# Values half a block later, and the round trip of 1/z a block later, in the attention stage of a decoder trunk

## The chip, the cores and the metric

One core of one Trainium2 chip runs the whole trunk as one program. The metric is the device time of one execution in microseconds (us). Before the change it is 2227.3 us, the median of three runs (2226.78 to 2228.44).

The engines go by the names of the profile: PE is TensorE (matmuls), PEld its weight loads, DVE is VectorE, ACT is ScalarE, POOL is GpSimd, SP is SyncE. Each engine takes its instructions in order. DMAs are issued from the queues of SP, ACT and POOL. An instruction that waits for another engine or for a DMA holds up everything behind it on its own engine or queue.

## What is computed

Two decoder layers over 1024 positions of width 1024 in float32: a short gated convolution with a SwiGLU FFN, then dilated attention with 16 heads of 64 and a second FFN, and a last RMSNorm. The change is in the attention layer:

```python
qkv = (h @ w_qkv).reshape(bsz, seq, 3, N_HEADS, HEAD_DIM)
q, k, v = qkv[:, :, 0], qkv[:, :, 1], qkv[:, :, 2]
for window, dilation in BRANCHES:          # (128, 1), (512, 4), (2048, 16)
    o, l = dilated_branch(q, k, v, rel_bias, window, dilation)
    ...
alpha = jax.nn.softmax(jnp.stack(lses, axis=0), axis=0)
o = jnp.sum(alpha[..., None] * jnp.stack(outs, axis=0), axis=0)
return o.reshape(bsz, seq, D_MODEL) @ w_out
```

The weighted sum of three softmaxes is one softmax over all the scores of the three branches. So per head the kernel needs the exponentials of all scores below one common maximum, their products with the values, the sum z of the exponentials, and a division by z. Then comes the output product with `w_out` and the addition to the residual x.

## The kernel before

All engines follow an order that the source writes out by hand. Matrix products in float32 are made of three products of rounded parts (`hi` and `lo`), so weights and activations are split first: ACT copies the high part (L141), DVE subtracts (L142).

The kernel has stages: convolution, first FFN, query and key products of pairs 0 to 5 by Strassen-like products, attention, second FFN. A pair is two heads. The attention stage (`attention`, L1465) begins with the values of group 0 (`value_tiles`, two tiles) and the strided key copies of head 0 (`classes`, L1539, on ACT). Then `slot` (L1721) is called 17 times, once for each head n and once more. In what follows a call of `slot` is a block; it is even or odd as n is.

A block before the change works like this:

- SP loads the bias of head n+1 (L1451, L1452) and its keys and queries (`load_kq`, L1529 to L1533: `ka`, `qa`, `ql`).
- First half: eight steps of `scores` of head n on PE (L1555, L1556), evicted with the bias by DVE (L1566 to L1597), with the maximum over keys at the end (DVE L1605, L1606, and on POOL `partition_all_reduce`, L1609, into `mb`). Between them run the products with the values of head n-1 (`values`, PE L1628), which need the exponentials `lf`, `lh`, `ld`, `lp` and the values `vx`. At their end ACT copies z and o out of PSUM (L1651, L1652).
- Second half, eight steps: mostly `dense` work, that is steps of other products that fill PE: value tiles of groups 1 to 3 (L1500 to L1502), query and key products of pairs 6 and 7 (`projections`, L369 to L371), and at last the output product over the first five pairs (`out_product`, L369 to L371). A block has 15 dense steps, the last four blocks 20. In step 1 and 2 are the key copies of head n+1; in step 4 (`SOFT`) the softmax of head n: DVE subtracts `mb` (L1617), ACT takes the exponential (L1618). In even blocks `load_values` (L1512) loads `vx` of the pair on SP; there is one buffer of it, so the load waits for the values of the pair before.
- 1/z: the sum z lies along the free dimension in two partitions. In the second half of an even block `finish` (L1655) writes z of the last pair to HBM (L1660), reads it back with 128 partitions (`zc`, L1663), has DVE take the reciprocal (L1665), writes it (L1666), and reads it back spread over 64 partitions a head (L1668). All four DMAs are on POOL. In step 2 of the next odd block `attended` (L1711) multiplies o with 1/z on DVE (L1715) and stores o (L1716).

A value tile's evictions are ACT's (L1505), and its store to HBM too (L1509). The stage's `first` part of the output product adds into x, which SP loads (L1797). The rest of the pairs follow in `group1` of the next stage (`by_columns`), once the last head is divided. `AO` says how many pairs go into the first part.

Of the kernel before, what the change touches and what calls it, by code (L numbers as in the profile page):

```python
# [17 lines left out]
S = 1024  # L18
D = 1024
DF = 2816  # L20
H = 16
# [24 lines left out]
SOFT = 4  # L46
FIN0 = 2
AO_WIDE = 5
AO = 5
FILL = (("v", 0), ("v", 1), ("v", 2), ("qk", 6), ("v", 3), ("qk", 7))  # L50
DEEP_ORDER = (1, 2, 5, 6, 7, 3, 4)


# [44 lines left out]
def trunk(ctx: ExitStack, tc: tile.TileContext, x, gains_in, cwi, ck, cwo, wqkv, wo, relb,  # L98
# [275 lines left out]
    def run(*gens):  # L374
        for _ in zip(*gens):
            pass
        for g in gens:
            for _ in g:
                pass
# [1085 lines left out]
    def attention(norm, qk):  # L1465
# [23 lines left out]
        def value_tiles(g, j):  # L1489

            if j == 0:
                wv[:] = [take(("v", g, i), 1) for i in range(2)]
            v = page("v")
            for b4 in range(4):
                t = 4 * j + b4
                b = bank()[:, :256]
                for k in range(KT):
                    (hi, lo), (whi, wlo) = qk.h[j][k], wv[k // 4]
                    a, c = slice(b4 * 128, b4 * 128 + 128), slice(k % 4 * 256, k % 4 * 256 + 256)
                    nc.tensor.matmul(b, hi[:, a], whi[:, c], start=k == 0, stop=False)  # L1500
                    nc.tensor.matmul(b, hi[:, a], wlo[:, c], start=False, stop=False)  # L1501
                    nc.tensor.matmul(b, lo[:, a], whi[:, c], start=False, stop=k == KT - 1)  # L1502
                    if k % 2:
                        yield
                nc.scalar.activation(v[:, b4 * 256:b4 * 256 + 256], b, AF.Identity, scale=norm.r[:, t:t + 1])  # L1505
                yield
            vd = vdram[g]
            for r in range(4):
                nc.scalar.dma_start(bass.AP(vd.tensor, vd.offset + (512 * j + r) * 256,  # L1509
                                          [[16 * 256, 32], [4 * 256, 4], [1, 256]]), v[32 * r:32 * r + 32])  # L1510

        def load_values(p):  # L1512
            src = vdram[p // 2]
            for a in range(2):
                off = src.offset + p % 2 * 128 + a * 64
                dims = slice(128 * a, 128 * a + 64)
                nc.sync.dma_start(vx[:, 0:8, dims], bass.AP(src.tensor, off, [[256, 128], [128 * 256, 8], [1, 64]]))
                for h in range(2):
                    nc.sync.dma_start(vx[:, 8 + 4 * h:12 + 4 * h, dims],
                                        bass.AP(src.tensor, off + 512 * 256 * h, [[1024, 128], [256, 4], [1, 64]]))  # L1520

        def load_kq(n):
# [12 lines left out]
        def classes(n):  # L1535

            KC[n] = page("kca", F32R)
            for h in range(2):
                nc.scalar.activation(KC[n][:, half(h)], view(KS[n], h * HALF, [[1, 4], [4, 128]]), AF.Copy)  # L1539
                yield  # L1540
# [114 lines left out]
        def finish(p):  # L1655

            o, z = OZ.pop(p)
            if p < NPAIR - 1:
                zd, rd = zdram[p]
                nc.gpsimd.dma_start(zd, z[0:65:64])  # L1660
                yield
                zc = scope["pool"].tile([128, 16], F32, name="zc", tag="zc", bufs=2)
                nc.gpsimd.dma_start(zc, bass.AP(zd.tensor, zd.offset, [[16, 128], [1, 16]]))  # L1663
                yield
                nc.vector.reciprocal(zc, zc)  # L1665
                nc.gpsimd.dma_start(bass.AP(rd.tensor, rd.offset, [[16, 128], [1, 16]]), zc)  # L1666
                yield
                nc.gpsimd.dma_start(z, bass.AP(rd.tensor, rd.offset, [[S, 2], [0, 64], [1, S]]))  # L1668
                yield
                put_off.append((p, o, z))  # L1670
                return

            zd, rd = zdram[p]
            wide = lambda t: bass.AP(t.tensor, t.offset, [[HALF, 2], [1, HALF]])
            thin = lambda t: bass.AP(t.tensor, t.offset, [[8, 128], [1, 8]])
            nc.gpsimd.dma_start(wide(zd), z[0:65:64, HALF:])
            zc = scope["pool"].tile([128, 8], F32, name="zl", tag="zl", bufs=1)
            nc.gpsimd.dma_start(zc, thin(zd))
            acts[p] = page("o_hi", F32R), page("o_lo", F32R)

            def scaled(c0, c1):
                q = slice(c0, c1)
                nc.vector.tensor_tensor(out=o[:, q], in0=o[:, q], in1=z[:, q], op=ALU.mult)

            def parts(h):
                split(o[:, half(h)], [t[:, half(h)] for t in acts[p]])

            for c in (0, 256):
                nc.vector.reciprocal(z[:, c:c + 256], z[:, c:c + 256])
                scaled(c, c + 256)  # L1690
                if c:
                    parts(0)
                    nc.scalar.activation(scratch, eps, AF.Sqrt)
                yield

            def rest():
                scaled(HALF, S)
                parts(1)

            last_part.append(rest)  # L1700
            yield
            ensure(ahead_ao + KT - AO_WIDE)
            nc.vector.reciprocal(zc, zc)
            nc.gpsimd.dma_start(thin(rd), zc)
            for a in range(2):
                nc.gpsimd.dma_start(z[64 * a:64 * a + 64, HALF:],
                                    bass.AP(rd.tensor, rd.offset + a * HALF, [[0, 64], [1, HALF]]))
            ensure(ahead_ao + KT - AO_WIDE + 4)
            yield
# [11 lines left out]
        def slot(n, dense, ndense, late=0, hook=iter(())):  # L1721

            def other(k):
                for _ in range(k):
                    next(dense, None)

            p, a = divmod(n, 2)
            if n < H:
                new = dict(bias=bias.pop(n))
                sc = scores(p, a, new)  # L1730
            else:
                sc = iter(())
            if n + 1 < H:
                bias[n + 1] = load_bias(n + 1)
                load_kq(n + 1)
            if n:
                q, b = divmod(n - 1, 2)
                if b == 0:
                    OZ[q] = page("o"), page("z")
                old = live.pop(n - 1)  # L1740
                old.update(o=OZ[q][0], z=OZ[q][1])
                pv = values(q, b, old)
            else:
                pv = iter(())
            extra = later = iter(())
            used = 0
            if a == 0 and n and not late:
                other(1)
                used += 1
            for i in range(8):  # L1750
                next(sc, None)
                next(pv, None)
                next(pv, None)
                if (i >= late if late else i < 3) and i % 2 == 0:
                    other(1)
                    used += 1
            run(sc)
            run(pv)
            if n + 1 < H:
                later = classes(n + 1)  # L1760
            if a == 0 and p:
                extra = finish(p - 1)
            if a == 0 and n < H:
                load_values(p)
            left = max(ndense - used, 0)
            for i in range(8):
                if a == 1 and i == 2:
                    attended()
                if i < FIN0 or i > SOFT:
                    next(extra, None)  # L1770
                if i in (1, 2):
                    next(later, None)
                if i == SOFT:
                    if n < H:
                        live[n] = new
                        run(softmax(new))
                if i >= SOFT:
                    next(hook, None)
                other(left * (i + 1) // 8 - left * i // 8)
            run(extra)  # L1780

        def load_attended(ps):
# [20 lines left out]
        X[:] = [None] * KT  # L1803
        bias = {0: load_bias(0)}
        load_kq(0)
        for j in range(2):
            run(value_tiles(0, j))
        run(classes(0))
        live = {}
        ahead_ao = [k for k, f in ops].index(("ao", 1, AO_WIDE - 1))  # L1810
        done, first = {}, {}
# [10 lines left out]
        def halves():  # L1822
            for q, t in done.items():
                first[q] = split(t)
                yield

        dense = fill()
        for n in range(H):
            if n == H - 4:
                done.update(load_attended(range(AO)))  # L1830
            hook = halves() if n == H - 4 else iter(())
            slot(n, dense, 20 if n > H - 4 else 15, 3 if n == H - 2 else 0, hook)
            run(hook)
        acts.update(split_attended(load_attended(range(AO, 7))))
        ensure(ahead_ao)
        slot(H, dense, 20)
        run(dense)
        return acts

# [198 lines left out]
```

## Time and profile before

| | us |
|---|---|
| median of three runs | 2227.3 |
| the profiled execution's own time | 2226.7 |
| its span, first to last instruction | 2224.7 |
| PE busy | 2125.2 |
| DVE busy | 1747.7 |
| ACT busy | 1007.3 |
| POOL busy | 234.5 |
| PE busy in the attention stage, 1118.5 to 1541.0 | 348.4 of 422.5 |
| mean granted clock there | 0.89 of full speed |

How to read the lines: a group of instructions is named by its line, engine, operation and tiles, out<-in. "A <- B: t, n, m" is a wait: A waited for B, t us in all, n times, m the longest. In a timeline a row has the start, the length, the engine and the instruction; brackets hold the idle time of the engine before it and what ended it. Stretches give the busy time of the engines, the granted clock of PE, the share of the 16 DMA engines that was busy, and the rate.

### The profile page before, as it was taken

To read this page: it belongs to the slowest core of one execution; us is meant where nothing else is said; L and a number is where in the kernel's file an instruction comes from. 1 tells how busy PE (TensorE), PEld (TensorE's weight loads), DVE (VectorE), ACT (ScalarE), POOL (GpSimd) and SP (SyncE) were. 2 spreads that over 40 slices of the span, in tenths; PEclk is the share of its full clock that TensorE was granted. 3 is DMA by queue.
4 is the path that set the end of the run, shared out by engine and by line. 5 is a ranking of instruction groups with operands and counts; after the bars stand their busy time and mean duration, and the time that the engine had idled before them with its cause. 6 is when DMAs were issued, how large, how long until landed. Compare 5 with 4: busy or idle time off the path is not lost.

```text
span 2224.7 us, 30938 instructions
## 1 busy us (share of the span) xinstructions
PE 2125.2 (96%) x11086; PEld 1823.8 (82%) x11086; DVE 1747.7 (79%) x3272; ACT 1007.3 (45%) x1848; POOL 234.5 (11%) x331
## 2 busy tenths in 40 slices
PE   9999999999999999999988777799999999999998
PEld 7788888888888888778888667688788888888887
DVE  8897679988888888689665554677898888888886
ACT  7433336434343554355444333434644444446435
POOL 1000000101010010002212121221001010101000
PEclk9999999999999999999999888899999999999999
DMA  7322643233333584326666554765322333367532
GB/s 218 86 86 76 222 147 86 90 105 105 106 104 112 198 232 140 123 96 203 212 152 160 137 140 119 202 181 177 81 95 100 109 105 105 109 198 220 173 97 76
DMA packets 152584, 304.92 MB, mean 137 GB/s; under 512 B 55102, under 2 KB 66606, under 8 KB 152432
## 3 DMA queue, kind: packets, MB, share of 16 engines
q1 hardware_dynamic: 107488, 201.94, 30.5%
q0 software_dynamic: 32704, 82.12, 11.5%
q10 hardware_dynamic: 12240, 18.90, 2.4%
q8 instruction: 88, 1.44, 0.3%
q14 instruction: 64, 0.52, 0.1%
HBM read 212.48 MB, written 83.05 MB: 133 GB/s over the span
## 4 chain that ended last, share of the span: by engine, by line
PE 82%; DVE 7%; DMA 6%; issue 3%; ACT 2%; POOL 1%; SPq 0%; ACTq 0%; DVEq 0%; POOLq 0%
PE bank L562 19%; PE bank L561 18%; PE bank L560 18%; DMA z<-rdram 3%; PE bank L1628 3%; PE bank L371 3%; PE bank L370 3%; PE bank L369 3%; PE bank L652 3%; PE bank L655 3%; PE bank L654 3%; DVE w L142 1%; PE bank L1556 1%; DVE b L553 1%; PE bank L1501 1%
## 5 line engine op out<-in xcount | busy, mean ns | idle before, releaser
L562 PE MATMUL bank<-b,w 128*128 128x512 f32 x1952 | 761.9, 390 | 5.9 <-DVE w L142 5.7
L560 PE MATMUL bank<-b,w 128*128 128x512 f32 x1952 | 764.2, 392 | 1.3 <-ACT w L141 1.1
L561 PE MATMUL bank<-b,w 128*128 128x512 f32 x1952 | 761.8, 390 | 2.6 <-DVE b L553 2.2
L562 PEld LDWEIGHTS bank<-b,w 128*128 128x128 f32 x1952 | 367.2, 188 | 86.0 <-DVE w L142 9.7
L561 PEld LDWEIGHTS bank<-b,w 128*128 128x128 f32 x1952 | 367.5, 188 | 79.6 <-DVE b L553 3.1
L560 PEld LDWEIGHTS bank<-b,w 128*128 128x128 f32 x1952 | 367.5, 188 | 78.3 <-ACT w L141 1.7
L141 ACT ACTIVATE w<-combo 128x512 fp32r<-128x512 f32 (+2 forms) x488 | 249.1, 540 | 230.7 <-DVE combo L189 207.3
L142 DVE TENSOR_TENSOR w<-combo,w 128x512 fp32r<-128x512 f32 (+2 forms) x488 | 277.7, 583 | 37.9 <-ACT w L141 37.2
L566 ACT ACTIVATE part<-bank 128x512 f32<-128x512 f32 x186 | 110.8, 596 | 390.1 <-PE bank L562 388.3
L142 DVE TENSOR_TENSOR w<-raw,w 128x512 fp32r<-128x512 f32 (+2 forms) x334 | 183.0, 569 | 35.9 <-ACT w L141 35.9
L570 DVE TENSOR_TENSOR part<-part,bank 128x256 f32<-128x256 f32 (+1 forms) x366 | 171.3, 499 | 31.1 <-PE bank L562 16.6
L141 ACT ACTIVATE w<-raw 128x512 fp32r<-128x512 f32 (+2 forms) x334 | 161.2, 525 | 45.1 <-PE bank L562 11.5
L369 PE MATMUL bank<-w_hi,w 128*128 128x512 f32 (+1 forms) x320 | 119.6, 374 | 0.0
L371 PE MATMUL bank<-w_hi,w 128*128 128x512 f32 (+1 forms) x320 | 117.8, 368 | 0.7 <-DVE w L142 0.7
L370 PE MATMUL bank<-w_lo,w 128*128 128x512 f32 (+1 forms) x320 | 117.7, 368 | 0.0
L790 DVE TENSOR_TENSOR x<-x,bank 128x512 f32<-128x512 f32 x136 | 93.4, 687 | 29.2 <-PE bank L562 29.2
L189 DVE TENSOR_TENSOR combo<-raw 128x512 f32<-128x512 f32 (+1 forms) x172 | 111.8, 650 | 0.0
L491 DVE TENSOR_TENSOR x<-x,bank 128x512 f32<-128x512 f32 (+1 forms) x104 | 66.3, 643 | 56.3 <-PE bank L371 55.7
L1628 PE MATMUL bank<-lf,vx 128*128 128x128 f32 x256 | 43.3, 324 | 53.4 <-ACT lf L1618 53.4
L553 DVE TENSOR_TENSOR b<-hin,b 128x512 fp32r<-128x512 f32 x126 | 79.8, 690 | 9.2 <-ACT b L552 9.1
L1628 PEld LDWEIGHTS bank<-lf,vx 128*128 128x128 f32 x256 | 39.9, 236 | 55.2 <-ACT lf L1618 54.9
L1500 PE MATMUL bank<-w_hi,b 128*128 128x256 f32 x256 | 76.3, 298 | 8.6 <-ACT w_hi L141 8.6
(252 smaller groups left out, 3688.9 us busy)
## 6 DMA issues: line engine op xcount, KB each, us to landing
hin<-part SPq DMA_DIRECT2D x126, 256.0 KB, 4.7
raw<-in_ffn_w_gate SPq DMA_DIRECT2D x44, 512.0 KB, 4.2
raw<-in_ffn_w_up SPq DMA_DIRECT2D x44, 512.0 KB, 4.6
part<-sum POOLq DMA_DIRECT2D x72, 256.0 KB, 2.3
raw<-in_ffn_w_down SPq DMA_DIRECT2D x48, 384.0 KB, 3.3
raw<-in_attn_w_qkv SPq DMA_DIRECT2D x27, 512.0 KB, 3.8
raw<-in_conv_w_in SPq DMA_DIRECT2D x24, 512.0 KB, 3.6
part<-part POOLq DMA_DIRECT2D x36, 256.0 KB, 2.4
```

The source lines that it names most:

```text
L141: nc.scalar.activation(hi, src, AF.Copy)
L142: eng.tensor_tensor(out=lo, in0=src, in1=hi, op=ALU.subtract)
L189: eng.tensor_tensor(out=c, in0=a, in1=b, op=op)
L369: nc.tensor.matmul(b, whi[:, a], ahi[:, s], start=first, stop=False)
L370: nc.tensor.matmul(b, whi[:, a], alo[:, s], start=False, stop=False)
L371: nc.tensor.matmul(b, wlo[:, a], ahi[:, s], start=False, stop=last)
L560: nc.tensor.matmul(b, hi[:, a], bhi, start=start and k == 0, stop=False, skip_group_check=True)
L561: nc.tensor.matmul(b, hi[:, a], blo, start=False, stop=False, skip_group_check=True)
L562: nc.tensor.matmul(b, lo[:, a], bhi, start=False, stop=k == n - 1, skip_group_check=True)
L566: nc.scalar.activation(t, b, AF.Copy)
L570: nc.vector.tensor_tensor(out=t, in0=t, in1=b, op=ALU.add)
L1628: nc.tensor.matmul(view(acc[ih], off, dims), vx[:, u, 64 * a:64 * a + 128], rhs, start=first, stop=last)
```

## The change

- In blocks up to 13 (`LAG`) the values of head n-1 run in the second half of block n and no longer beside the scores. The eight dense steps that this frees go between the scores, seven stay between the values.
- There, `finish` of the last pair runs in the odd block: the store of z and its reading back between the scores, the reciprocal and its store at the start of the second half, the spread of 1/z in step 4. `attended` follows in step 2 of the next even block. The spread is issued by SP.
- `load_values` is issued by ACT, in blocks up to 13 at the start of an odd block.
- Key copies are in steps 0 and 1; the softmax in step 3.
- The output product takes 4 pairs in the attention stage and 4 behind it (`AO`). All blocks have 15 dense steps. Query and key products of pair 7 go ahead of value group 3. The stored pairs are loaded back in block 12, as before.
- The key copies of head 0 go between the value tiles ahead of the first block.

```diff
@@ -46,8 +46,9 @@
 SOFT = 4
 FIN0 = 2
 AO_WIDE = 5
-AO = 5
-FILL = (("v", 0), ("v", 1), ("v", 2), ("qk", 6), ("v", 3), ("qk", 7))
+AO = 4
+LAG = 13
+FILL = (("v", 0), ("v", 1), ("v", 2), ("qk", 6), ("qk", 7), ("v", 3))
 DEEP_ORDER = (1, 2, 5, 6, 7, 3, 4)
 
 
@@ -1514,9 +1515,9 @@
             for a in range(2):
                 off = src.offset + p % 2 * 128 + a * 64
                 dims = slice(128 * a, 128 * a + 64)
-                nc.sync.dma_start(vx[:, 0:8, dims], bass.AP(src.tensor, off, [[256, 128], [128 * 256, 8], [1, 64]]))
+                nc.scalar.dma_start(vx[:, 0:8, dims], bass.AP(src.tensor, off, [[256, 128], [128 * 256, 8], [1, 64]]))
                 for h in range(2):
-                    nc.sync.dma_start(vx[:, 8 + 4 * h:12 + 4 * h, dims],
+                    nc.scalar.dma_start(vx[:, 8 + 4 * h:12 + 4 * h, dims],
                                         bass.AP(src.tensor, off + 512 * 256 * h, [[1024, 128], [256, 4], [1, 64]]))
 
         def load_kq(n):
@@ -1665,7 +1666,7 @@
                 nc.vector.reciprocal(zc, zc)
                 nc.gpsimd.dma_start(bass.AP(rd.tensor, rd.offset, [[16, 128], [1, 16]]), zc)
                 yield
-                nc.gpsimd.dma_start(z, bass.AP(rd.tensor, rd.offset, [[S, 2], [0, 64], [1, S]]))
+                nc.sync.dma_start(z, bass.AP(rd.tensor, rd.offset, [[S, 2], [0, 64], [1, S]]))
                 yield
                 put_off.append((p, o, z))
                 return
@@ -1743,40 +1744,58 @@
             else:
                 pv = iter(())
             extra = later = iter(())
+            lagged = n <= LAG
+            if n + 1 < H:
+                later = classes(n + 1)
+            if lagged and a and p:
+                extra = finish(p - 1)
             used = 0
-            if a == 0 and n and not late:
-                other(1)
-                used += 1
+            if lagged:
+                if a:
+                    load_values(p)
+                for i in range(8):
+                    next(sc, None)
+                    if n or i % 2:
+                        other(1)
+                        used += 1
+                    if i in (0, 3):
+                        next(extra, None)
+                run(sc)
+            else:
+                if a == 0 and not late:
+                    other(1)
+                    used += 1
+                for i in range(8):
+                    next(sc, None)
+                    next(pv, None)
+                    next(pv, None)
+                    if i >= late and i % 2 == 0:
+                        other(1)
+                        used += 1
+                run(sc)
+                run(pv)
+                if a == 0:
+                    extra = finish(p - 1)
+                if a == 0 and n < H:
+                    load_values(p)
+            left = max(ndense - used, 0)
             for i in range(8):
-                next(sc, None)
                 next(pv, None)
                 next(pv, None)
-                if (i >= late if late else i < 3) and i % 2 == 0:
-                    other(1)
-                    used += 1
-            run(sc)
-            run(pv)
-            if n + 1 < H:
-                later = classes(n + 1)
-            if a == 0 and p:
-                extra = finish(p - 1)
-            if a == 0 and n < H:
-                load_values(p)
-            left = max(ndense - used, 0)
-            for i in range(8):
-                if a == 1 and i == 2:
+                if i == 2:
                     attended()
-                if i < FIN0 or i > SOFT:
+                if i in (0, 4) if lagged else i < FIN0 or i > SOFT:
                     next(extra, None)
-                if i in (1, 2):
+                if i in (0, 1):
                     next(later, None)
-                if i == SOFT:
+                if i == (3 if lagged else SOFT):
                     if n < H:
                         live[n] = new
                         run(softmax(new))
                 if i >= SOFT:
                     next(hook, None)
                 other(left * (i + 1) // 8 - left * i // 8)
+            run(pv)
             run(extra)
 
         def load_attended(ps):
@@ -1803,9 +1822,12 @@
         X[:] = [None] * KT
         bias = {0: load_bias(0)}
         load_kq(0)
-        for j in range(2):
-            run(value_tiles(0, j))
-        run(classes(0))
+        run(value_tiles(0, 0))
+        early = classes(0)
+        for i, _ in enumerate(value_tiles(0, 1)):
+            if i in (10, 14):
+                next(early)
+        run(early)
         live = {}
         ahead_ao = [k for k, f in ops].index(("ao", 1, AO_WIDE - 1))
         done, first = {}, {}
@@ -1826,14 +1848,14 @@
 
         dense = fill()
         for n in range(H):
-            if n == H - 4:
+            if n == LAG - 1:
                 done.update(load_attended(range(AO)))
-            hook = halves() if n == H - 4 else iter(())
-            slot(n, dense, 20 if n > H - 4 else 15, 3 if n == H - 2 else 0, hook)
+            hook = halves() if n == LAG - 1 else iter(())
+            slot(n, dense, 15, 3 if n == H - 2 else 0, hook)
             run(hook)
         acts.update(split_attended(load_attended(range(AO, 7))))
         ensure(ahead_ao)
-        slot(H, dense, 20)
+        slot(H, dense, 15)
         run(dense)
         return acts
 
```

## The prediction

> **What bounds the kernel now.** I read the page first, then who waited for whom, then the order of time around one long wait.
>
> ```profile
> PE 2125.2 (96%) x11086; PEld 1823.8 (82%) x11086; DVE 1747.7 (79%) x3272; ACT 1007.3 (45%) x1848; POOL 234.5 (11%) x331
> PEclk9999999999999999999999888899999999999999
> ```
>
> PE is busy for 96% of the span, so only what makes PE idle or slow is worth anything; the granted clock sags in one place alone, the middle of the span. That is the attention stage, some 1113 to 1541 us. Of it, the waits of PE:
>
> ```profile
> PE bank L1628 <- ACT lf L1618: 53.4, 7, 14.9
> PE bank L1500 <- ACT w_hi L141: 8.6, 1, 8.6
> PE bank L369 <- ACT w_hi L141: 5.0, 1, 5.0
> PE bank L1555 <- ACT kca L1539: 4.6, 1, 4.6
> PE bank L370 <- DVE w_lo L142: 3.1, 2, 2.5
> ```
>
> The value products (L1628) wait seven times, 53.4 us, for the exponential (L1618). Why the exponential is late is seen in the rows around one such wait, of DVE, ACT and PE in turn:
>
> ```profile
> 1253.28 1.23 DVE L1715 TENSOR_TENSOR o<-o,z 128x1024 f32<-128x1024 f32 x1 [15.57 <-DMA z<-rdram]
> 1254.42 1.22 DVE L142 TENSOR_TENSOR w_lo<-raw,w_hi 128x1024 fp32r<-128x1024 f32 x1
> 1255.56 1.22 DVE L1617 TENSOR_TENSOR lf<-lf,mb 128x1024 f32<-128x1024 f32 x1
> ...
> 1256.81 1.06 ACT L1618 ACTIVATE lf<-lf 128x1024 f32<-128x1024 f32 x1 [16.30 <-DVE lf L1617]
> ...
> 1257.91 0.58 PE L1628 MATMUL bank<-lf,vx 128*128 128x128 f32 x1 [14.95 <-ACT lf L1618]
> ```
>
> DVE runs in order. It stands 15.57 us at the product with 1/z, waiting for z's spread; the maximum is subtracted only behind it, then the exponential, then PE. So the root is not the softmax but the transfer of 1/z:
>
> ```profile
> DVE o L1715 <- DMA z<-rdram: 61.6, 7, 16.0
> POOL zc L1663 <- DMA zdram<-z: 35.9, 7, 6.5
> DVE zc L1665 <- DMA zc<-zdram: 27.9, 7, 5.6
> POOL z L1668 <- DMA rdram<-zc: 16.6, 6, 4.8
> ```
>
> **What the removed waits are worth.** If the exponential is ready before PE comes to the values, 53.4 us go. Behind a wait PE is also slow (three stretches, columns: length, busy time of PE, PEld, DVE, ACT, POOL, granted clock, DMA share, GB/s, the third with PE alone; then the first and the last of six waits of PE at the values that are over 2.5 us):
>
> ```profile
> 1257.00:1261.00 4.00, 3.08 (x11) 2.86 (x12) 3.55 (x5) 3.79 (x6) 0.00 (x0) 0.50 0.08 32
> 1261.00:1265.00 4.00, 4.00 (x31) 3.89 (x30) 3.10 (x7) 0.22 (x1) 1.09 (x2) 0.88 0.34 131
> ...
> 1393.00:1397.00 4.00, 4.00 (x16) 0.50 0.98 237
> ...
> 1135.72 0.58 PE L1628 MATMUL bank<-lf,vx 128*128 128x128 f32 x1 [2.53 <-ACT lf L1618]
> ...
> 1418.80 0.41 PE L1628 MATMUL bank<-lf,vx 128*128 128x128 f32 x1 [3.05 <-ACT lf L1618]
> ```
>
> After the wait that ended at 1257.91 PE was busy 3.08 us at 0.50 and 4.00 us at 0.88: 3.08 x 0.50 + 4.00 x 0.12 = 2.0 us of work lost. The third row stands behind a wait of about 3 us, and is at 0.50 too, so I give 2.0 us to each of the six waits: 12 us. [...]
>
> The first scores wait 4.6 us for the strided key copies (L1539). The change emits these copies between the value tiles of the start; I take all of the 4.6 (bounds: 0, if the keys land late as well, and 4.6). Removed: 53.4 + 12 + 4.6 = 70 us.
>
> **Does the new order hide 1/z?** A block is one call of slot, one head. Undisturbed blocks:
>
> ```profile
> 1189.00:1241.00 52.00, 52.00 (x426) 50.94 (x426) 32.84 (x64) 24.28 (x36) 12.47 (x8) 1.00 0.56 138
> ...
> 1201.74 1.23 DVE L1617 TENSOR_TENSOR lf<-lf,mb 128x1024 f32<-128x1024 f32 x1 [0.29 <-POOL mb L1609]
> ...
> 1220.87 1.22 DVE L1617 TENSOR_TENSOR lf<-lf,mb 128x1024 f32<-128x1024 f32 x1 [3.43 <-POOL mb L1609]
> ...
> 1223.74 1.15 DVE L1617 TENSOR_TENSOR lp<-lp,mb 128x384 f32<-128x384 f32 x2
> ...
> 1229.86 1.42 DVE L1566 TENSOR_TENSOR lf<-bank,bias 128x256 f32<-128x256 f32 x4
> ...
> 1237.02 0.69 DVE L1606 TENSOR_TENSOR m<-m,lp 128x512 f32<-128x512 f32 x1
> ```
>
> Here PE had no gap for 52 us at clock 1.00, and a block took 1220.87 - 1201.74 = 19.1 us. Half of it, 9.5 us, is my estimate for each half of a new block. The values now come 9.5 us later, so the exponential has that much more slack. The chain of 1/z in an odd block, from its start, with the means of the rows above and the copies below: four copies of z and o, 4 x 0.59 = 2.4; zdram 35.9/7 = 5.1; zc 27.9/7 = 4.0, so 11.5 plus issues of some 0.6 each, 12.7. The write of 1/z stands on POOL behind the maximum of the block, which starts at about 9.5 and takes some 3.4, so 13; with 16.6/6 = 2.8 and an issue SyncE has z's spread at about 17.
>
> ```profile
> L1651 ACT ACTIVATE z<-bank x32: 589/593/599, 1145.6 to 1530.9; 64x512 f32<-64x512 f32 x32
> ...
> L1668 POOL DMA_DIRECT2D z<-rdram x7: 822/822/822, 1186.9 to 1500.5; - x7
> ...
> DMA to landing us min/median/max: 12.8/16.7/21.0
> ...
> 1459.00:1460.00 1.00, 1.00 (x11) 1.00 0.13 53
> ```
>
> The last row is a stretch in which z's spread runs alone (columns: length, PE, clock, DMA share, GB/s): a share of 0.13 is 2 of 16 engines, and 512 KB at 53 GB/s are 9.9 us. That is most of the 12.8, and it is the two engines, not the queue, so SyncE will not make it much shorter. At 12.8 it lands at 30, which is 10.9 into the next block; the product with 1/z is due at 9.5 plus a quarter of 9.5, 12. So it lands in time. At 21.0 DVE would stand 7 us, which the 9.5 of slack still cover.
>
> **What is added.** Bounds first, then what I take.
>
> ```profile
> ka<-kq SPq DMA_DIRECT2D x32, 256.0 KB, 7.4
> ...
> vx<-vdram SPq DMA_DIRECT2D x32, 128.0 KB, 4.1
> ...
> SPq L1517 <- PE bank L1628: 71.4, 6, 20.7
> ...
> SPq L1530 <- DMA vdram<-v: 10.7, 2, 6.0
> ...
> L1519 SPq DMA_DIRECT2D vx<-vdram x32: 539/628/8050, 1121.3 to 1487.0; - x32
> ...
> L1539 ACT ACTIVATE kca<-ka x32: 1094/1124/1178, 1116.8 to 1488.2; 128x512 fp32r<-128x512 f32 x32
> ```
>
> Values on ScalarE: six DMAs a pair, about 6 x 0.6 = 3.6 us of its sequencer, which is free of exponentials then. SyncE is rid of a place where it stood 71.4 us for PE. They are issued behind the z and o copies, at 2.4 us of the odd block; the second one is what the first products need: 2.4 + 1.2 + 4.1 = 7.7, due at 9.5. [...] Behind these DMAs ScalarE has evictions of value tiles and key parts, for which PE has spare banks.
>
> SyncE now stands at z's spread until 17 us of an odd block. Behind it are the bias, ka, qa and ql of the next head but one; ka lands at 30 plus some 2.5, and two copies of 1.12 end at 35; its scores start at 38. Slack 3 us; I take 0 (bounds: 0, and the rival below).
>
> The output product, 4+4 pairs for 5+3:
>
> ```profile
> 1535.68 0.39 PE L369 MATMUL bank<-w_hi 128*128 128x512 f32 x1
> 1535.91 0.39 PE L370 MATMUL bank<-w_lo,w_hi 128*128 128x512 f32 x1
> ...
> 1536.36 0.39 PE L369 MATMUL bank<-w_hi 128*128 128x512 f32 x1
> ```
>
> A step of three matmuls is 0.68 us. 16 steps leave the attention stage and come back in the product behind it: -10.9 + 10.9 = 0. The last three blocks then have 15 steps instead of 20 as cover, 3.4 us less each, with 1/z of pair 6 still on its old plan; I take 3 us (0 to 3 x 3.4). The 8.6, 5.0 and 3.1 us of PE behind weight splits stay: the same splits still stand behind the exponentials where a new group starts.
>
> Sum, against the profiled execution's own 2226.7 (span 2224.7 plus 2.0; 0.6 below the median of 2227.3, so I leave it): 2226.7 - 70 + 7 + 3 = 2167 us.
>
> **The rivals.**
> - *All hidden.* The weight waits of 8.6 + 5.0 + 3.1 = 16.7 go as well, with their slow clock (three times 2.0 us), and the added 7 is 2: 2167 - 16.7 - 6 - 5 = 2139. For it: 52 us with no gap in the old order. Against it: ScalarE still comes to the splits behind the exponentials.
> - *DVE sets the pace.* The scores' share of a block is 1229.86 to 1237.71, 7.9 us, the wait for the maximum 3.43, the softmax 1220.87 to 1224.89, 4.0, so 15.3 of 19.1 are a loop, and evictions, splits and the product with 1/z come on top. If each of 16 blocks loses 2 us there: 2167 + 32 = 2199. Against it: DVE waits for PE in the quiet blocks.
> - *Slower: SyncE's loads stick behind z's spread.* The place is the SyncE queue of each odd block. If the spread takes its 21.0 and ka its whole 7.4 behind it, the copies end at 17 + 21.0 + 7.4 + 2.2 = 47.6 against 38.2: 9.4 us late in each of 7 pairs, and 2.0 of clock: 80 us, so 2247. It decides from a lateness of 60/7 - 2 = 6.6 us a pair, that is from 25 us between the spread's issue and ka. For it: the two engines, 9.9 us. Against it: the spread goes first in SyncE's queue now, so nothing of that queue can lengthen it. [...]
>
> **How the numbers follow.** My sum 0.55; all hidden 0.16; DVE's pace 0.20; SyncE's loads 0.07; no change to speak of 0.02. The range 2138 to 2202 reaches from the second to the third and leaves out the last two and the tails. Below 0.2% (4.5 us) a change of this kernel can't be told from none. Faster 0.91, same 0.02, slower 0.07.
>
> **What would show it.** PE's wait at the values for lf below 10 us, DVE's wait for z<-rdram below 15; clock near 1.0 across the stage; z's spread near 13 us. Wrong if PE waits at L1555 or L1556 for kca, qa or ql, if vx releases the values, or if ScalarE's DMAs stand long for SyncE's.

## The result, and the profile after

The changed kernel takes 2199.6 us (median of 4 runs, 2198.0 to 2200.6), against 2227.9 for the kernel before (2226.8 to 2228.6): a ratio of 0.9873, with a 95% interval of 0.9856 to 0.9890. That is 28 us gained, where 60 were forecast. The time lies near the upper end of the range, and at the 2199 of the second rival; the experiments show that it got there by another way.

The page of the changed kernel, its busy line and its clock:

```profile
PE 2121.2 (96%) x11086; PEld 1817.0 (83%) x11086; DVE 1746.1 (79%) x3272; ACT 1006.7 (46%) x1848; POOL 228.5 (10%) x324
PEclk9999999999999999999999999899999999999999
```

The sag in the middle is flatter, but still there. The stretch of 440 us that holds the attention stage shows how much of it (columns as in the prediction: length, busy time of PE, PEld, DVE, ACT, POOL, clock, DMA share, GB/s); first the kernel before:

```profile
1100.00:1540.00 440.00, 361.21 (x2497) 338.46 (x2497) 257.69 (x452) 172.62 (x250) 83.88 (x71) 0.90 0.59 157
```

and the changed one:

```profile
1100.00:1540.00 440.00, 382.01 (x2590) 351.03 (x2589) 275.48 (x483) 183.06 (x269) 81.43 (x69) 0.94 0.62 168
```

PE was idle for 440 - 361.2 = 78.8 us, and is idle for 58.0. So some 21 us of idleness went. The clock, 0.94 for 0.90, brought less: for the same number of matmuls PE's busy time fell by 4.0 us over the whole execution, 2125.2 to 2121.2. With 21.9 us less idleness these are the 25.9 us between the two spans, 2224.7 and 2198.8. But a wait of 53.4 us was to go. The waits of PE after (line waiting, what it waited for, us in total, times, longest) show that it did go, and what came:

```profile
PE bank L370 <- ACT w_hi L142: 13.7, 2, 12.7
PE bank L1556 <- ACT kca L1540: 8.2, 2, 4.9
PE bank L1556 <- DMA qa<-kq: 5.4, 1, 5.4
PE bank L1501 <- ACT w_hi L142: 5.4, 1, 5.4
PE bank L370 <- ACT w L142: 4.9, 1, 4.9
PE bank L1556 <- DVE lp L1618: 4.8, 1, 4.8
...
PE bank L1629 <- ACT lf L1619: 2.2, 2, 1.7
PE bank L1557 <- DMA ql<-kq: 2.1, 3, 1.1
```

(Lines behind the head of the file have moved by one: L1628 is now L1629.) The value products wait 2.2 us for the exponential, where they waited 53.4: the lag does what it says. In its place PE waits at the first scores of a head (L1556, L1557) for kca, qa and ql, the key copies and loads of that head, 15.7 us together, and longer than before at a weight split, 12.7 us at one place. The prediction had named the first as what would prove it wrong. Rows of the waits of SyncE's queue and of DVE tell why those are late:

```profile
SPq L1669 <- DMA rdram<-zc: 87.0, 7, 22.0
SPq L156 <- DMA z<-rdram: 24.4, 3, 9.9
...
SPq L1533 <- DMA z<-rdram: 16.8, 2, 10.8
SPq L1452 <- DMA z<-rdram: 12.4, 1, 12.4
```

```profile
DVE o L1716 <- DMA z<-rdram: 18.1, 5, 5.8
```

SyncE stands 87 us ahead of the spread until 1/z is written, and 53.6 us more at later DMAs until the spread has landed. One pair in order of time, rows of PE, ACT, POOL, DVE and SP from the timeline of the changed kernel:

```profile
1216.18 0.39 PE L1556 MATMUL bank<-qa,kca 128*128 128x256 f32 x1 [3.25 <-ACT kca L1540]
...
1220.87 0.59 ACT L1652 ACTIVATE z<-bank 64x512 f32<-64x512 f32 x1
...
1222.97 0.56 POOL L1661 DMA_DIRECT2D zdram<-z  x1 [14.04 <-ACT z L1652]
1228.29 0.57 POOL L1664 DMA_DIRECT2D zc<-zdram  x1 [4.77 <-DMA zdram<-z]
1231.22 1.23 DVE L143 TENSOR_TENSOR w_lo<-raw,w_hi 128x1024 fp32r<-128x1024 f32 x1 [4.92 <-ACT w_hi L142]
1234.46 3.22 POOL L1610 PARTITION_ALL_REDUCE mb<-m  x1 [5.60 <-DVE zc L1666]
1237.56 0.56 POOL L1667 DMA_DIRECT2D rdram<-zc  x1
...
1239.39 0.56 SPq L1669 DMA_DIRECT2D z<-rdram  x1
...
1242.55 0.58 SPq L1531 DMA_DIRECT2D ka<-kq  x1
...
1256.46 1.24 SPq L156 DMA_DIRECT2D raw<-in_attn_w_qkv  x2
...
1260.36 2.10 ACT L1540 ACTIVATE kca<-ka 128x512 fp32r<-128x512 f32 x2 [14.61 <-DMA ka<-kq]
...
1262.95 0.55 PE L1556 MATMUL bank<-qa,kca 128*128 128x256 f32 x1 [5.36 <-DMA qa<-kq]
```

Counted from the start of the odd block at 1216.2: the copies of z begin at 4.7 (the exponentials of the block before stand ahead of them on ScalarE), the maximum holds POOL from 18.3 to 21.4, the write of 1/z goes behind it, and the spread is issued at 23.2. SyncE's eighth DMA behind the spread, a weight load, is issued only at 40.3; the profile has it wait 9.9 us for the spread, which so took at most 17.1 us. The keys of the next head, issued 3.2 us behind the spread, are in hand at 44.2, that is 17.8 us after their issue (the median of such a load was 7.4 in the kernel before). In the next two odd blocks the same time, from issue to copy, is 18.9 and 17.9 us. PE comes to the scores at 41.4 and stands 5.36.

The 3.25 us at the head of these rows belong to the pair before. ScalarE had stood there at issuing four writes of values, 6 us behind that pair's spread (1191.42), but it was free again at 1210.7. The key copies began only at 1215.03, after 4.32 us more:

```profile
1197.70 12.35 ACTq L1510 DMA_DIRECT2D vdram<-v  x4
...
1215.03 2.12 ACT L1540 ACTIVATE kca<-ka 128x512 fp32r<-128x512 f32 x2 [4.32 <-DMA bias<-tables]
```

So a load ended last there, not ScalarE's stand. The profile names the bias, which the copies don't read; the keys had been issued 2.9 us behind that spread, and no view shows when they landed. As to the stand itself, the third of the writes went out at 1207.77, 0.9 us after SyncE, standing for the spread, had gone on (1206.84). So the two stands end close together; the profile doesn't name what ScalarE stood for, and whether it was the spread is not shown.

### The profile page after: what moved, and what is told of

The parts are those of the page before. It is cut to its first block, busy times and chain, and to the rows that moved or that the text cites. A ratio compares the mean times of both kernels' runs of the same rounds, so it can differ in the third digit from the quotient of the medians.

```text
span 2198.8 us, 30951 instructions
## 1 busy us (share of the span) xinstructions
PE 2121.2 (96%) x11086; PEld 1817.0 (83%) x11086; DVE 1746.1 (79%) x3272; ACT 1006.7 (46%) x1848; POOL 228.5 (10%) x324
## 5 line engine op out<-in xcount | busy, mean ns | idle before, releaser
L143 DVE TENSOR_TENSOR w<-raw,w 128x512 fp32r<-128x512 f32 (+2 forms) x342 | 188.5, 572 | 46.9 <-ACT w L142 46.9
L571 DVE TENSOR_TENSOR part<-part,bank 128x256 f32<-128x256 f32 (+1 forms) x366 | 170.6, 495 | 31.2 <-PE bank L563 16.7
L142 ACT ACTIVATE w<-raw 128x512 fp32r<-128x512 f32 (+2 forms) x342 | 167.1, 530 | 52.3 <-PE bank L563 12.2
L370 PE MATMUL bank<-w_hi,w 128*128 128x512 f32 (+1 forms) x400 | 153.9, 385 | 18.6 <-ACT w_hi L142 13.7
L371 PE MATMUL bank<-w_lo,w 128*128 128x512 f32 (+1 forms) x400 | 150.2, 375 | 1.6 <-DVE w_lo L143 1.6
L372 PE MATMUL bank<-w_hi,w 128*128 128x512 f32 (+1 forms) x400 | 149.9, 375 | 1.1 <-DVE w L143 1.1
L370 PEld LDWEIGHTS bank<-w_hi,w 128*128 128x128 f32 x400 | 75.9, 190 | 32.4 <-ACT w_hi L142 14.1
L371 PEld LDWEIGHTS bank<-w_lo,w 128*128 128x128 f32 x400 | 76.0, 190 | 15.6 <-DVE w_lo L143 2.9
L372 PEld LDWEIGHTS bank<-w_hi,w 128*128 128x128 f32 x400 | 75.8, 190 | 15.4 <-DVE w L143 2.1
```

The source lines that it names most:

```text
L142: nc.scalar.activation(hi, src, AF.Copy)
L143: eng.tensor_tensor(out=lo, in0=src, in1=hi, op=ALU.subtract)
L370: nc.tensor.matmul(b, whi[:, a], ahi[:, s], start=first, stop=False)
L371: nc.tensor.matmul(b, whi[:, a], alo[:, s], start=False, stop=False)
L372: nc.tensor.matmul(b, wlo[:, a], ahi[:, s], start=False, stop=last)
L571: nc.vector.tensor_tensor(out=t, in0=t, in1=b, op=ALU.add)
```

## The experiments

Each run is the changed kernel (or the kernel before, where said) with one edit; ratios are against the kernel before on the same chip.

**The lag taken back**, with the old order of the fillers (no_lag; lines that only let it run without lagged blocks are left out here):

```diff
-LAG = 13
+LAG = -1
-FILL = (("v", 0), ("v", 1), ("v", 2), ("qk", 6), ("qk", 7), ("v", 3))
+FILL = (("v", 0), ("v", 1), ("v", 2), ("qk", 6), ("v", 3), ("qk", 7))
...
```

> The changed kernel without the half block of lag and with the old order of the two fillers: values behind the scores in the same half, 1/z a block earlier; z's spread on SyncE, value loads on ScalarE, four pairs in the first group and the early key copies stay. If the lag brought what was gained: PE's waits for lf come back (40 to 60 us with 12 of clock), 2225 to 2260. If the queues brought it: 2190 to 2205.

2233.8 us, ratio 1.0035 (1.0020 to 1.0050): the rest of the change without the lag is slower than no change. The waits of PE:

```profile
PE bank L1629 <- ACT lf L1619: 27.2, 9, 6.0
PE bank L1556 <- DVE lp L1618: 13.3, 3, 6.7
```

The waits for the exponential are back, though half as long, and the waits for loads are there on top. So the lag brought the gain; that the moves of queues took from it is seen in lag_only below.

**z's spread back to POOL's queue** (z_pool), and **in two DMAs by partitions** (z_two), two ways of taking it out of SyncE's way:

```diff
-                nc.sync.dma_start(z, bass.AP(rd.tensor, rd.offset, [[S, 2], [0, 64], [1, S]]))
+                nc.gpsimd.dma_start(z, bass.AP(rd.tensor, rd.offset, [[S, 2], [0, 64], [1, S]]))
```

> The changed kernel with only z's spread given back to POOL's queue. Theory A (SyncE stands eight hardware DMAs later for the spread's semaphore, 10 to 17 us a pair, and the loads of the next head but one come late): SyncE's waits for z<-rdram go, PE's waits for kca, qa, ql, lp (18 us) and most of the 12.7 us for w_hi go with them, and some 2 us of clock each: 2160 to 2180 us. Theory B (what costs is that the spread itself lands late or crowds two engines, whoever issues it): 2193 to 2205. Theory C (DVE's and ScalarE's work sets the pace of a block): 2195 to 2203.

```diff
-                nc.sync.dma_start(z, bass.AP(rd.tensor, rd.offset, [[S, 2], [0, 64], [1, S]]))
+                for i in range(2):
+                    nc.sync.dma_start(z[64 * i:64 * i + 64], bass.AP(rd.tensor, rd.offset + i * S, [[0, 64], [1, S]]))
```

> The changed kernel with z's spread on SyncE as two DMAs of 64 partitions each, whose slowest dimension is 64 and no longer 2. Theory A: the spread lands in some 4 to 6 us instead of 10 to 17, its semaphore is free before SyncE comes to it again, DVE's 18 us for z<-rdram fall below 3, PE's waits for kca, qa, ql, lp go and the 12.7 us for w_hi shrink: 2155 to 2175. Theory B expects the same here. Theory C: 2193 to 2202.

z_pool: 2181.0 us, ratio 0.9794 (0.9771 to 0.9818). z_two: 2151.6 us, ratio 0.9656 (0.9637 to 0.9674). C falls with both. A has z_pool 1 us above its numbers, and z_two below the 2155 it allowed: taking the spread off SyncE is worth 19 us, making it short 48, so B has a share as well. The DMA issue row of the spread, the largest waits of PE and the stretch of the stage in z_two:

```profile
z<-rdram SPq DMA_DIRECT2D x14, 256.0 KB, 3.4
```

```profile
PE bank L1501 <- ACT w_hi L142: 5.4, 1, 5.4
PE bank L370 <- ACT w_hi L142: 4.6, 2, 4.0
PE bank L1556 <- DVE lf L1567: 3.4, 2, 2.3
```

```profile
1100.00:1540.00 440.00, 419.46 (x2806) 383.56 (x2805) 322.43 (x558) 218.71 (x328) 89.35 (x75) 0.98 0.65 176
```

A half of the spread lands in 3.4 us (the last number of the first row, the median from issue where the profile shows the landing), no wait for kca, qa or ql is left among the large ones, the split at L370 costs 4.6 for 13.7, and PE is idle for 20.5 us of the stage.

**Is it the number of engines, or just two smaller DMAs?** z_cols cuts the same spread by columns, which leaves two rows as the slowest dimension:

```diff
+                for i in range(2):
+                    nc.sync.dma_start(z[:, half(i)], bass.AP(rd.tensor, rd.offset + i * HALF, [[S, 2], [0, 64], [1, HALF]]))
```

> The changed kernel with z's spread in two DMAs again, but cut by columns: each has 128 partitions of 512 and still two rows as its slowest dimension. If two engines are what makes the spread long: as after, 2193 to 2206, and DVE's wait for z stays near 18. If two smaller DMAs are enough: 2150 to 2170.

2194.9 us, ratio 0.9860 (0.9837 to 0.9882): within the first number, and 43 us behind z_two, which moves the same bytes in as many DMAs. DVE's wait for z fell, to 10.6 us where some 18 were expected, but the loads behind the spread are nearly as late (ScalarE waits 47.4 us for ka, 53.4 in the changed kernel):

```profile
PE bank L1556 <- DMA qa<-kq: 9.3, 3, 3.5
```

So the way it is cut decides. This fits the two engines that the prediction worked out from a share of 0.13; the changed kernel has 0.13 too, at 55 GB/s, from 1389 to 1393, while SyncE stands for the spread. The engines of the halves by themselves were not measured.

**The loads' place behind the spread, or SyncE's stand for it?** Both A's reason (SyncE stands for the spread at later DMAs, 53.6 us in all) and the place of the loads behind the spread in SyncE's queue fit so far. z_after issues the same long spread behind the loads of the next head:

```diff
-                nc.sync.dma_start(z, bass.AP(rd.tensor, rd.offset, [[S, 2], [0, 64], [1, S]]))
+                spreads.append((z, rd))
...
                 load_kq(n + 1)
+            while spreads:
+                z, rd = spreads.pop()
+                nc.sync.dma_start(z, bass.AP(rd.tensor, rd.offset, [[S, 2], [0, 64], [1, S]]))
```

> The changed kernel with z's spread (one DMA, still on SyncE) issued behind the loads of the next head instead of ahead of them. Theory R (the loads lie behind the spread's bytes on two engines, in the order of SyncE's ring): ka lands some 7 us after its issue instead of 18, PE's waits at the first scores of odd heads (3.3, 5.4, 1.1, 4.9, 4.8 us) go, the spread lands some 5 us later, which the lag covers: 2178 to 2192. Theory S (SyncE and ScalarE stand at the spread's semaphore, whatever the order): the same waits a head later, 2196 to 2210.

2177.0 us, ratio 0.9784 (0.9758 to 0.9810), just below R's numbers and far from S's. Rows of SP and ACT, then SyncE's and DVE's largest waits for z:

```profile
1227.63 2.25 SPq L1531 DMA_DIRECT2D ka<-kq  x1
...
1235.38 0.56 SPq L1739 DMA_DIRECT2D z<-rdram  x1
...
1238.34 2.17 ACT L1540 ACTIVATE kca<-ka 128x512 fp32r<-128x512 f32 x2
```

```profile
SPq L1819 <- DMA z<-rdram: 20.3, 2, 12.0
```

```profile
DVE o L1716 <- DMA z<-rdram: 33.7, 6, 9.4
```

The keys are copied with no wait, while SyncE still stands for the spread, 20.3 us at L1819 and 30.5 in all (53.6 in the changed kernel), and DVE stands longer for z than there. So most of what SyncE's move cost was that loads came behind the spread, not SyncE's stand for it. The edit changes two things at once: the loads stand neither behind the spread any more nor behind SyncE's wait for 1/z. In z_two SyncE still waits 79.7 us for 1/z with the loads behind, and PE has no such wait; so that alone does not make PE stand. The keys took 17.8 us from issue to copy behind the spread in the changed kernel; ahead of it, here, they are copied 10.7 us after their issue.

z_pool speaks for order rather than crowding. There a load of keys went out at 1329.45, while the spread in POOL's queue was under way (issued at 1320.69, waited for by DVE until 1335.69). PE stands for none of these loads, and the landings of the keys that its profile shows are all short:

```profile
DMA to landing us min/median/max: 4.4/6.1/6.9
```

z_after keeps one long wait of PE amid the scores of a head, 5.94 us at 1348.92, for which the profile names no releaser. DVE had stood 9.37 us for z until 1342.99 and began to take that head's scores out of PSUM only at 1348.08; so this looks like the old chain through DVE and not like a wait for loads.

**The value loads back to SyncE** (vx_sp), and **both queue moves taken back** (lag_only):

```diff
-                nc.scalar.dma_start(vx[:, 0:8, dims], bass.AP(src.tensor, off, [[256, 128], [128 * 256, 8], [1, 64]]))
+                nc.sync.dma_start(vx[:, 0:8, dims], bass.AP(src.tensor, off, [[256, 128], [128 * 256, 8], [1, 64]]))
...
-                    nc.scalar.dma_start(vx[:, 8 + 4 * h:12 + 4 * h, dims],
+                    nc.sync.dma_start(vx[:, 8 + 4 * h:12 + 4 * h, dims],
```

> The changed kernel with the six value loads of a pair back on SyncE. If ScalarE's stands at its own value loads cost PE (the 4.9 us for w behind them, 2.9 us for vx): 2185 to 2197. If SyncE then stands for PE at them with bias, ka and qa behind, as in the kernel before (71 us of SyncE): 2205 to 2230.

> The changed kernel with both queue moves undone: z's spread on POOL, value loads on SyncE; lag, four pairs in the first group, filler order and early key copies stay. If the two moves cost separately (18.6 us by z_pool, 8.3 by vx_sp): 2168 to 2178. If value loads on SyncE make it stand for PE once the spread is out of its way: 2185 to 2205.

vx_sp: 2191.3 us, ratio 0.9835 (0.9817 to 0.9853), 8 us less than the changed kernel and inside the first numbers. lag_only: 2178.3 us, ratio 0.9788 (0.9769 to 0.9807), just outside the 2168 to 2178; the two costs don't add up, since z_pool has 2181.0 already. Together the two moves cost 2199.6 - 2178.3 = 21 us. With neither, there is still one large wait. Rows of DVE, ACT and PE in lag_only:

```profile
1382.65 1.22 DVE L1716 TENSOR_TENSOR o<-o,z 128x1024 f32<-128x1024 f32 x1 [11.66 <-DMA z<-rdram]
...
1388.68 1.04 ACT L142 ACTIVATE w_hi<-oin 128x1024 fp32r<-128x1024 f32 x1
...
1389.77 0.80 PE L370 MATMUL bank<-w_hi,w 128*128 128x512 f32 x1 [12.56 <-ACT w_hi L142]
```

It is the old chain once more: DVE stands at the product with 1/z, the exponentials are late, and this time it is not the values that wait for them (they lag) but the first split of the output product, which stands behind them on ScalarE. In the changed kernel ScalarE comes late to the same split because it waits for ka:

```profile
1404.10 2.10 ACT L1540 ACTIVATE kca<-ka 128x512 fp32r<-128x512 f32 x2 [14.55 <-DMA ka<-kq]
```

SyncE stood there at the bias load of that head for the spread (the 12.4 us above). Either way it is the long spread; z_two has 4.0 us at this place.

**Is the lag needed, if the spread is short?** The kernel before with nothing changed but the spread in two DMAs on POOL (before_two):

```diff
-                nc.gpsimd.dma_start(z, bass.AP(rd.tensor, rd.offset, [[S, 2], [0, 64], [1, S]]))
+                for i in range(2):
+                    nc.gpsimd.dma_start(z[64 * i:64 * i + 64], bass.AP(rd.tensor, rd.offset + i * S, [[0, 64], [1, S]]))
```

> The kernel before, with nothing changed but z's spread on POOL as two DMAs of 64 partitions instead of one of 128. If the spread's 12.8 to 21 us on two engines are the whole root: each of the seven waits of DVE for z (61.6 us) loses about 10 us, PE's 53.4 us for lf fall below 10 and the clock's 12 go with them: 2165 to 2185 us. If the half block of lag is needed all the same (the four copies, zdram and zc of 1/z still take 12.7 us before the spread): 2195 to 2220.

2178.2 us, ratio 0.9787 (0.9771 to 0.9803): the first theory's time. Two lines in place of one bring more than the whole change did. PE's wait for the exponential is down, but not below the 10 us expected:

```profile
PE bank L1628 <- ACT lf L1618: 12.1, 7, 2.8
```

These are seven short waits of 1 to 2.8 us. The next experiment shows what the lag is worth beside the short spread: two_pool_vx differs from before_two by the lag and the changes of order that come with it (four pairs, fillers, key copies), and takes 28 us less.

**Short spread without the queue moves, and with one of them** (two_pool_vx: z_two's edit on POOL, with the values on SyncE; z_two_vx: z_two's edit on SyncE, with the values on SyncE):

> Both queue moves undone, and z's spread in two DMAs of 64 partitions on POOL. If SyncE as the issuer is worth something once the spread is short (POOL's queue has the maximum and the projections' writes ahead of it): 2152 to 2162. If the queue doesn't matter then: 2145 to 2151, as z_two_vx has.

> Both at once: z's spread on SyncE in two DMAs of 64 partitions, and the value loads on SyncE. If the value loads on ScalarE cost by themselves: 2151.6 less about 8, 2140 to 2147. [...] If SyncE stands for PE at them: 2158 to 2185.

2150.5 us, ratio 0.9656 (0.9635 to 0.9677), and 2148.4 us, ratio 0.9650 (0.9635 to 0.9664). Once the spread is short no difference is seen between the queues that issue it, and the value loads on ScalarE cost some 3 us by the medians of z_two and z_two_vx; these three kernels can't be told apart by their intervals. z_two_vx is the fastest by its median, 51 us ahead of the changed kernel. Its page and its stage:

```profile
PE 2106.4 (98%) x11086; PEld 1807.7 (84%) x11086; DVE 1747.7 (81%) x3272; ACT 1008.0 (47%) x1848; POOL 231.8 (11%) x324
```

```profile
1100.00:1540.00 440.00, 420.06 (x2823) 384.87 (x2822) 325.66 (x563) 220.63 (x332) 89.79 (x75) 0.98 0.66 176
```

**The early key copies taken back**, in the changed kernel (no_early) and in z_two (two_no_early):

```diff
-        run(value_tiles(0, 0))
-        early = classes(0)
-        for i, _ in enumerate(value_tiles(0, 1)):
-            if i in (10, 14):
-                next(early)
-        run(early)
+        for j in range(2):
+            run(value_tiles(0, j))
+        run(classes(0))
```

> The changed kernel with the key copies of head 0 back behind the value tiles of the start. If they were worth what the prediction took (4.6 us of PE and 2.0 of clock): the wait at the first scores is back, 2204 to 2208. If the time only moves to the next wait: 2197 to 2202.

> z_two with the key copies of head 0 back behind the value tiles. If the 4.6 us were lost in later waits for SyncE's loads in the changed kernel: now that these are gone they count, 2156 to 2160. If they are worth nothing anyway: 2149 to 2154.

no_early takes 2200.0 us, ratio 0.9880 (0.9864 to 0.9896): no difference from the changed kernel. The wait is back, and the kernel makes it up; these are the first scores of head 0 and of head 11, the second to be held against 1359.48 and 4.82 us in the changed kernel:

```profile
1117.52 0.58 PE L1556 MATMUL bank<-qa,kca 128*128 128x256 f32 x1 [4.86 <-ACT kca L1540]
...
1359.31 0.55 PE L1556 MATMUL bank<-qa,kca 128*128 128x256 f32 x1 [4.37 <-DVE lp L1618]
```

What PE gains at the start it loses at the waits for loads, whose time is set by 1/z and SyncE. two_no_early takes 2157.9 us, ratio 0.9689 (0.9664 to 0.9714), 6 us more than z_two by the medians; the intervals overlap, so this points to a worth of about what was predicted rather than proving it.

Not tried: five pairs in the first group with the lag, since the fifth pair's product is not written when that group starts. So what 4+4 alone costs stays open.

## Why the prediction was off, point by point

- **What bounds the kernel before** was read rightly: the transfer of 1/z, on two engines by its share of 0.13. before_two shows the transfer's part with nothing else changed: 2178.2 us. The prediction stopped a step short: it took the two engines as given, "so SyncE will not make it much shorter", where cutting the spread by partitions does.
- **The 53.4 us for the exponential** went but for 2.2. Right, though DVE still stands 18.1 us for z, more than the 15 that the prediction gave as a sign; the slack of the exponential covers that.
- **The clock's 12 us** came in part: PE's busy time fell by 4.0 us, and the clock is 0.94 where near 1.0 was to be seen. The new waits slow PE as the old ones did: in the stretch from 1263 to 1267, behind the 5.36 us, the clock is 0.50. With most of them gone, in z_two, it is 0.98 over the stage.
- **The 4.6 us of the first scores** went, but were worth nothing here: a later wait with a date of its own took them back. Removed ahead of a chain that sets the pace, this wait was no gain (no_early 2200.0 us against 2199.6).
- **The value loads on ScalarE**: the 7 us in the sum were the author's estimate, and no run shows them as such. What the runs showed in their place is 8.3 us (vx_sp, 2191.3 for 2199.6), so right in size. But the price hangs on the long spread: with the spread short (z_two 2151.6 against z_two_vx 2148.4), or out of SyncE's queue (z_pool 2181.0 against lag_only 2178.3), it is some 3 us by the medians.
- **"Slack 3 us; I take 0"** is the step that failed, in the paragraph on SyncE's standing at the spread. Its dates were too early. The spread was to be issued at 17 us of the odd block, and was at 23.2 in the pair above: the copies of z were put at the block's start instead of behind the exponentials (4.7), and the maximum at 9.5 instead of 18.3. PE had done its scores by 9.1, so the half block was right for PE. But DVE, which evicts them, stood 4.92 us at a weight split for ScalarE (the row at 1231.22), and ScalarE had itself stood at its DMA issues, first at the value loads. So in this pair one queue move made the other later: in vx_sp, with the value loads on SyncE, DVE stands 1.82 us there and the spread goes at 20.0 (in the next three pairs it gains 2.5 us or less). The landing was taken as 12.8, the shortest of the kernel before; here SyncE could go on 14.9 to 18.4 us behind it in six pairs, around the median of 16.7 in the prediction's own row. With the median alone the copies end at 17 + 16.7 + 2.5 + 2.2 = 38.4, and the slack is gone. So the copies of the keys, due at 38 and forecast for 35, ended at 46.3 against a due date of 41.4.
- **The third rival**, SyncE's loads stuck behind the spread, is therefore what came, at its named place: the keys took 17.8 us behind the spread (1242.55 to 1260.36), and z_after, which puts them ahead of it, takes 2177.0 us. Its price was too high (5.36 us late at this pair, for 9.4) and it did not turn the sign, but it should have stood in the sum. The second rival, which has the measured time, is not what happened: z_two, with the same instructions on DVE, is 48 us faster.
- **"The 8.6, 5.0 and 3.1 us of PE behind weight splits stay"** failed at one of them: 8.6 became 5.4, but the split in the first output group grew from 5.0 to 12.7, since it stands behind exponentials and key copies that wait for the same spread.
- **The tail's 3 us**: behind the last lagged block PE waits 4.9 us at one weight split, which on ScalarE stands behind key copies that waited 9.79 us for DMAs, and 1.7 us at most elsewhere. So more than 3 us was lost there, in part to late loads and not to the thinner cover; the term was not measured alone.

The sum without the queue moves would have been 2226.7 - 70 + 3 = 2160, and lag_only has 2178: the wait at the split is the largest single part, 12.6 us where 5.0 were counted, and the rest is spread over the clock, 0.95 there, and waits that no run singles out. The moves then cost 21 us, where 7 were taken.

## What to carry to other kernels

A transfer that everything waits for is looked at first by its own pattern: here a share of DMA engines of 0.13 while it ran alone was the hint that another cut may make it shorter, and that alone was worth more than the schedule that hides it (before_two 2178.2 us against the changed kernel's 2199.6). Before a long transfer is moved into a queue, the loads behind it are dated with its longest landing (21.0 us here, not 12.8), and its start with everything that stands ahead of it on each engine, not from the start of its block. Slack that was taken from a wait, the 4.6 us of the first scores, was no gain here while later waits had a date of their own (no_early 2200.0 us against 2199.6).

## What the hardware showed that was not expected

The 512 KB of the spread take 12.8 to 21.0 us as one DMA of two rows by 64 partitions (the kernel before). As two DMAs of one row by 64 each, from the same queue (before_two), the halves land like this:

```profile
DMA to landing us min/median/max: 3.5/4.2/6.6
```

Halves by columns are no remedy (z_cols, 2194.9 us where z_two takes 2151.6). And the clock fell behind a wait shorter than any that the prediction showed; the stretch behind the 2.32 us wait of PE that ended at 1134.49 in the changed kernel:

```profile
1134.49 0.35 PE L1556 MATMUL bank<-qa,ka 128*128 128x256 f32 x1 [2.32 <-DVE lf L1567]
```

```profile
1134.00:1138.00 4.00, 3.51 (x18) 3.41 (x19) 3.97 (x11) 1.46 (x5) 0.00 (x0) 0.66 0.73 170
```

The granted clock is 0.66 there; it was 1.00 from 1130 to 1132.
